# Low parts of summed weight blocks made by a negated cast and an adding DMA

## Chip, cores and metric

One core of a Trainium2 chip runs the kernel. The metric is device time in microseconds (us), the median of three executions: 2752.41 us before (2750.66 to 2753.99). The engines are called PE (TensorE), DVE (VectorE), ACT (ScalarE), POOL (GpSimd) and SP (SyncE), as in the profile.

## What is computed

The reference is one encoder block on 512 tokens with a model width of 2048:

```python
proj = rmsnorm(x, norm1_w) @ w_in          # 2048 x 9248
# 8 heads of gated DeltaNet and 8 heads of HGRN2, both directions, on columns of proj
x = x + y @ w_out                          # 2048 x 2048
h2 = rmsnorm(x, norm2_w)
x = x + (silu(h2 @ w_gate) * (h2 @ w_up)) @ w_down   # 2048 x 5632 twice, 5632 x 2048
return rmsnorm(x, norm_f_w)
```

Four stages are large matrix products: the projections by `w_in`, the output projection by `w_out`, gate and up, and the last product, "down", by `w_down`. Between the first two the heads are scanned.

## The kernel before

**The products.** Each large product is done with seven block products in place of eight (`PRODUCTS`). A **unit** is one call of `block_weights` (L957 to L978) with the matmuls that use its result. It loads 2 x 256 KB of weights into the tile `raw` by two DMAs of SP's queue, and DVE makes four blocks of sums of them in `wsum` (L972 to L974). Three raw blocks and four summed blocks are then split into a high part (`whi`, ACT casts the fp32 values to the rounded type fp32r, L976) and a low part (`wlo`, DVE subtracts the high part from the value, L977). The activations are split in the same way (`oh` and `ol`; in the projections `xh`, `xl` and `tp`). A block product is then three matmuls: high by high, high by low, low by high (L1000 to L1004). A full unit has 2 x 7 x 3 = 42 matmuls of 128x256. In the last two row blocks of down one unit in three is half as large.

**The loops.** `projections` (L313 to L427) walks over 36 groups of columns, four units each: 144 units. The output projection has 32, gate and up 176, down 96 (16 of them half units). After the last unit of a group `combine` (L1010 to L1023) adds the seven results up on DVE; in the projections the result `t` is multiplied by the row factors `rb` (L421; on POOL for the kinds k, q and v, on DVE for the others) and goes through convolution, activation and stores. POOL also multiplies in the convolution (L337), in the gates (L395) and in the preparation of the DeltaNet heads (L473, L485).

**What sets the order.** A framework schedules each engine's instructions by the program's order, priorities and its own estimate of when data are ready; the engines then run their lists in order. `block_weights` runs at a raised priority in the projections (`whead`). The pools give three buffers to `raw` and two each to `wsum`, `whi` and `wlo`, so the casts of a unit wait until the matmuls of the unit two before it have read the old contents.

Of the kernel before, what the change touches and what calls it, by code (L numbers as in the profile page):

```python
# [9 lines left out]
F32 = mybir.dt.float32  # L10
F32R = mybir.dt.float32r
U8 = mybir.dt.uint8
AF = mybir.ActivationFunctionType
ALU = mybir.AluOpType
# [3 lines left out]
P = 128  # L18
# [52 lines left out]
class Block:  # L71
# [3 lines left out]
        self.dram = ctx.enter_context(tc.tile_pool(name="dram", bufs=1, space=DRAM))  # L75

    whead = 0

    def split_act(self, src, hi, lo):
        nc = self.nc  # L80
        nc.scalar.copy(out=hi, in_=src)
        nc.vector.tensor_tensor(out=lo, in0=src, in1=hi.bitcast(F32), op=ALU.subtract)
# [230 lines left out]
    def projections(self, xops, chunk, tmp):  # L313
        nc, a = self.nc, self.a
# [83 lines left out]

        offs = dict(k=OFF_K, q=OFF_Q, v=OFF_V, z=OFF_Z, g=OFF_G, Q=OFF_QB, F=OFF_FF, B=OFF_FB, I=OFF_I)
        pend = [None, self.gates_b]  # L400
        prep = {}
        for h in range(H):
            prep.setdefault(self.PREP[h], []).append(self.gdn_head(h))
# [2 lines left out]
        n = 0  # L406
        while n < len(self.AHEAD):
            now = self.AHEAD[n:n + (2 if n == len(self.AHEAD) - 2 else 1)]
            todo = [f for m in range(n, n + len(now))
                    for f in ([pend.pop(0)] if pend else []) + ({2: [self.gates_c], 3: [self.gates_d]}.get(m, [])) + prep.get(m, [])]  # L410
            todo = [f for f in todo if f]
            prev = self.banks
            mats = [(w, (offs[kind] + g * 256, offs[kind] + g * 256 + P)) for kind, g in now]
            prods = self.block_products(mats, 0, xops, (lambda: [f(prev) for f in todo]) if todo else None, 4,
                                        before=None if n else chunk)
            self.whead = 2000
            for prod, (kind, g) in zip(prods, now):
                t = tmp.tile([P, 2, 2, ht], F32, name="t", bufs=2)
                self.combine(prod, t, tmp, 1, "comb")
                t = t.rearrange("p n h t -> p n (h t)")  # L420
                (nc.gpsimd if kind in "kqv" else nc.vector).tensor_tensor(  # L421
                    out=t, in0=t, in1=self.rb.unsqueeze(1).broadcast_to([P, 2, T]), op=ALU.mult)
                pend.append(post(kind, g, t))
            n += len(now)
        for todo in pend:
            if todo:
                todo(None)  # L427


    PREP = (18, 19, 20, 21, 23, 24, 25, 26, 22, 27)  # L430
# [366 lines left out]
    def mixers(self):  # L797
        tc = self.tc

        for n, count, shape in (("d_x0", 8, [2, P, T]), ("d_q", 4, [2, P, T]), ("d_k", 4, [2, P, T]), ("d_v", 4, [2, P, T]), ("d_g", 8, [2, P, T]),  # L800
                                ("d_hq", 4, [2, P, T]), ("d_hf", 8, [2, P, T]), ("d_hv", 4, [2, P, T]), ("d_L", 4, [2, P, 2 * T]),
                                ("d_y", 4, [4, P, T])):
            setattr(self, n, [self.dram.tile(shape, F32, name=f"{n}{i}") for i in range(count)])
        self.d_s = []
        self.banks = None
        self.wpairs, self.wbufs = 2, (3, 2, 2)
        with ExitStack() as st:
            pool = lambda name, **k: st.enter_context(tc.tile_pool(name=name, bufs=1, **k))
            early = pool("tmp0")
            acts, rest, self.smallp, self.wst = (pool(n) for n in ("acts", "tmp1", "small", "wst1"))  # L810
            tmp = Pools(rest, **{n: early for n in ("acc", "sq", "sh", "sl")})
            tops = Pools(None, **{f"tp{j}": pool(f"top{j}", side="right") for j in range(8)})
            self.ps = Banks([pool(f"ps1{i}", space=PSUM) for i in range(4)], ((0, 1), (2, 3)))
            self.tmp = tmp
            self.projections(*self.activations(tops, acts, tmp), tmp)
        self.scan()
# [140 lines left out]
    def block_weights(self, src, col):  # L957


        nc = self.nc  # L960
        n, m = src.shape[1] // 2, self.wpairs
        bufs = self.wbufs
        cut = lambda t, x: t[:, :x * n].rearrange("p (x j) n -> p x j n", j=n)
        raw = cut(self.wst.tile([P, 4 * m, P], F32, name="raw", bufs=bufs[0]), 4)
        sm = cut(self.wst.tile([P, 4 * m, P], F32, name="wsum", bufs=bufs[1]), 4)
        h = cut(self.wst.tile([P, 7 * m, P], F32R, name="whi", bufs=bufs[2]), 7)
        l = cut(self.wst.tile([P, 7 * m, P], F32R, name="wlo", bufs=bufs[2]), 7)
        with self.tc.high_priority(offset=self.whead):
            for r, c in ((2, col[0]), (0, col[1])):
                nc.sync.dma_start(out=raw[:, r:r + 2].rearrange("p k j n -> p (k j) n"), in_=src[:, :, c:c + P])  # L970
            tt = nc.vector.tensor_tensor
            tt(out=sm[:, 0:2], in0=raw[:, 0:1].broadcast_to([P, 2, n, P]), in1=raw[:, 2:0:-1], op=ALU.add)  # L972
            tt(out=sm[:, 2], in0=sm[:, 1], in1=raw[:, 2], op=ALU.add)  # L973
            tt(out=sm[:, 3], in0=sm[:, 2], in1=raw[:, 3], op=ALU.add)  # L974
            for o, src_ in ((slice(0, 3), raw[:, 1:]), (slice(3, 7), sm)):
                nc.scalar.copy(out=h[:, o], in_=src_)  # L976
                nc.vector.tensor_tensor(out=l[:, o], in0=src_, in1=h[:, o].bitcast(F32), op=ALU.subtract)  # L977
        return h, l  # L978

    def block_products(self, mats, k0, ops, between=None, at=2, order=None, before=None):  # L980


        nc = self.nc
        todo = []
        for w, col in mats:
            self.banks = self.ps.take(4, [P, 2, self.HT])
            todo.append((w.rearrange("(kt p) n -> p kt n", p=P), col, [self.banks[i // 2][:, i % 2] for i in range(7)], self.banks))
        n = KT // 2 if before else len(ops)
        starts = order or range(0, n, self.wpairs)
        for nb, j0 in enumerate(starts):  # L990
            m = min(self.wpairs, n - j0)
            if before is not None:
                before(nb)
            for v, col, prod, _ in todo:
                h, l = self.block_weights(v[:, k0 + 2 * j0:k0 + 2 * (j0 + m)], col)
                for j in range(m):
                    xh, xl = ops[j0 + j]
                    st, en = nb == 0 and j == 0, nb == len(starts) - 1 and j == m - 1
                    begun = set()
                    for wi, xi, i in self.PRODUCTS:  # L1000
                        mm = lambda a, b, s, e: nc.tensor.matmul(prod[i], lhsT=a, rhs=b, start=s, stop=e, skip_group_check=True)  # L1001
                        mm(h[:, wi, j], xh[xi], st and i // 2 not in begun, False)
                        begun.add(i // 2)
                        mm(h[:, wi, j], xl[xi], False, False)  # L1004
                        mm(l[:, wi, j], xh[xi], False, en)
            if between is not None and nb == (at - 1) // self.wpairs:
                between()
        return [banks for _, _, _, banks in todo]
# [125 lines left out]
    def run(self):  # L1134
        tc, st = self.tc, self.ctx
        pool = lambda name, where=st, side="right", **k: where.enter_context(
            tc.tile_pool(name=name, bufs=1, reuse_waits="tile", **(dict(side=side) if side else {}), **k))
        self.constants()
        self.mixers()
        self.ps = Banks([pool(f"ps{i}", side=None, space=PSUM) for i in range(4)], ((0, 2), (1, 3)))  # L1140
        self.wpairs, self.wbufs = 2, (3, 2, 2)
        self.wst = pool("wst")
        self.io = pool("io")
        self.ops = [pool("ops0", side="left"), pool("ops1", side="left")]
        self.ops.append(self.ops[1])
        with ExitStack() as ffn:
            self.ops.append(pool("ops3", ffn))
            self.sums = pool("sums", ffn)
            self.xops = []
            with ExitStack() as late:  # L1150
                token_scale = self.out_proj(pool("late", late))
            tio = pool("tio", side="left")
            self.gate_up(token_scale, pool("tb", ffn))
        self.down(tio, pool("more", side="left"), pool("accs"), pool("dtmp"))


# [19 lines left out]
```

## Time and profile before

| | |
|---|---|
| median of three executions | 2752.41 us |
| the profiled execution: its time | 2746.68 us |
| its span, first to last instruction | 2744.9 us |
| busy in the span: PE, DVE, ACT, POOL | 2520.9, 2506.7, 1282.1, 296.4 us |
| mean granted TensorE clock | 0.963 of 2.4 GHz |
| DMA read and written, mean rate | 361.89 MB, 132 GB/s |

An engine's busy time is the time in which it runs an instruction. Matmuls are pipelined, and the profile models their ends, so a stretch in which PE reads as busy throughout can still be slower than PE at its peak; the spacing of the matmuls tells that. The stages of this kernel follow one another, so each is read from its own stretch of the span: the projections fill it up to about 892 us, the scans lie between 892 and 1201 us, output projection, gate and up between 1201 and 2265 us, and down follows to the end.

### The profile page before, as it was taken

What the parts mean: (1) busy time and instruction counts of PE and PEld (TensorE: products, weight loads), DVE (VectorE), ACT (ScalarE), POOL (GpSimd) and SP (SyncE); (2) the same over time, 40 slices, a digit from 0 to 9 for tenths busy, and PEclk for the clock granted to TensorE, in tenths of its full rate; (3) what the DMA queues carried; (4) which work ended last, traced back from release to release, by engine and by line L of the source; (5) the groups of instructions that cost most, each with busy time, mean ns of one, the idle gap of its engine ahead of it and who ended that gap; (6) DMA issues with size and microseconds to landing.
All of it is one profiled execution on the core that took longest, in us unless ns stands there. A gap on an engine that the chain in (4) does not pass through costs nothing.

```text
span 2744.9 us, 55187 instructions
## 1 busy us (share of the span) xinstructions
PE 2520.9 (92%) x22511; PEld 2449.8 (89%) x22511; DVE 2506.7 (91%) x3978; ACT 1282.1 (47%) x1777; POOL 296.4 (11%) x148
## 2 busy tenths in 40 slices
PE   6999999888899587889999999999999999899996
PEld 5989999888899476789899999999999999898996
DVE  8999999998999887889998989999899999999996
ACT  6555655445454443444644434344433443444444
POOL 0121112223112554210000000000000000000000
PEclk9999999999999798999999999999999999999998
DMA  6334344556444643546434443434344364434333
GB/s 185 109 101 130 109 132 111 164 156 167 118 143 135 203 134 90 166 145 181 147 114 128 121 124 116 123 119 121 116 124 123 110 200 144 131 106 126 107 93 100
DMA packets 562345, 361.89 MB, mean 132 GB/s; under 512 B 51393, under 2 KB 514683, under 8 KB 562091
## 3 DMA queue, kind: packets, MB, share of 16 engines
q1 hardware_dynamic: 543515, 311.70, 39.6%
q10 hardware_dynamic: 18576, 46.67, 4.8%
q8 instruction: 176, 2.88, 0.4%
q14 instruction: 78, 0.64, 0.1%
HBM read 303.66 MB, written 54.62 MB: 131 GB/s over the span
## 4 chain that ended last, share of the span: by engine, by line
PE 49%; DVE 15%; issue 6%; DMA 4%; ACT 2%; POOL 1%; POOLq 0%; SPq 0%; ACTq 0%; DVEq 0%
PE big L1001 46%; DVE wlo L977 4%; DVE ol L954 1%; DVE wsum L972 1%; DVE wsum L974 1%; DMA L<-d_L 1%; DVE wsum L973 1%; ACT whi L976 1%; POOL acc L473 1%; DVE X L744 1%; DVE X L746 1%; DMA acc<-d_rows 0%; DVE lt L517 0%; DVE tsum L937 0%; PE oT L628 0%
## 5 line engine op out<-in xcount | busy, mean ns | idle before, releaser
L1001 PE MATMUL big<-oh,whi 128*128 128x256 f32 x4144 | 1139.1, 284 | 31.7 <-ACT whi L976 21.1
L1001 PE MATMUL big<-ol,whi 128*128 128x256 f32 x4144 | 1139.5, 282 | 1.8 <-DVE ol L954 1.6
L1001 PE MATMUL big<-oh,wlo 128*128 128x256 f32 x4144 | 1070.6, 283 | 16.8 <-DVE wlo L977 16.4
L1001 PEld LDWEIGHTS big<-oh,whi 128*128 128x128 f32 x4144 | 783.5, 190 | 42.4 <-ACT whi L976 28.8
L976 ACT CAST whi<-raw 128x768 fp32r<-128x768 f32 (+1 forms) x448 | 368.9, 824 | 907.3 <-PE big L1001 649.9
L1001 PEld LDWEIGHTS big<-ol,whi 128*128 128x128 f32 x4144 | 785.6, 190 | 3.3 <-DVE ol L954 2.8
L1001 PEld LDWEIGHTS big<-oh,wlo 128*128 128x128 f32 x4144 | 746.7, 190 | 22.6 <-DVE wlo L977 21.8
L977 DVE TENSOR_TENSOR wlo<-wsum,whi 128x1024 fp32r<-128x1024 f32 (+1 forms) x448 | 542.1, 1210 | 9.5 <-ACT whi L976 9.3
L976 ACT CAST whi<-wsum 128x1024 fp32r<-128x1024 f32 (+1 forms) x448 | 462.0, 1032 | 151.2 <-DVE wsum L974 148.1
L977 DVE TENSOR_TENSOR wlo<-raw,whi 128x768 fp32r<-128x768 f32 (+1 forms) x448 | 432.7, 966 | 85.9 <-ACT whi L976 82.2
L1001 PE MATMUL big<-tp,whi 128*128 128x256 f32 x2304 | 415.0, 286 | 27.9 <-ACT whi L976 17.0
L1001 PEld LDWEIGHTS big<-tp,whi 128*128 128x128 f32 x2304 | 348.5, 193 | 33.6 <-ACT whi L976 19.6
L972 DVE TENSOR_TENSOR wsum<-raw 128x512 f32<-128x512 f32 (+1 forms) x448 | 313.3, 700 | 10.2 <-DMA raw<-in_w_in 3.1
L1001 PE MATMUL big<-tp,wlo 128*128 128x256 f32 x1152 | 293.5, 290 | 21.7 <-DVE wlo L977 21.4
L1001 PE MATMUL big<-xh,whi 128*128 128x256 f32 x864 | 246.1, 289 | 10.4 <-ACT whi L976 7.3
L1001 PE MATMUL big<-xl,whi 128*128 128x256 f32 x864 | 244.8, 287 | 0.0
L1001 PE MATMUL big<-xh,wlo 128*128 128x256 f32 x864 | 229.3, 287 | 4.6 <-DVE wlo L977 4.3
L1001 PEld LDWEIGHTS big<-tp,wlo 128*128 128x128 f32 x1152 | 206.8, 195 | 28.8 <-DVE wlo L977 28.3
L974 DVE TENSOR_TENSOR wsum<-wsum,raw 128x256 f32<-128x256 f32 (+1 forms) x448 | 206.9, 463 | 2.4
L973 DVE TENSOR_TENSOR wsum<-wsum,raw 128x256 f32<-128x256 f32 (+1 forms) x448 | 189.4, 424 | 3.6
L1001 PEld LDWEIGHTS big<-xh,whi 128*128 128x128 f32 x864 | 167.7, 194 | 12.3 <-ACT whi L976 8.4
L1001 PEld LDWEIGHTS big<-xl,whi 128*128 128x128 f32 x864 | 166.7, 193 | 0.5
(302 smaller groups left out, 2628.2 us busy)
## 6 DMA issues: line engine op xcount, KB each, us to landing
raw<-in_w_in SPq DMA_DIRECT2D x288, 256.0 KB, 3.4
raw<-in_w_gate SPq DMA_DIRECT2D x176, 256.0 KB, 3.3
raw<-in_w_up SPq DMA_DIRECT2D x176, 256.0 KB, 3.4
raw<-in_w_down SPq DMA_DIRECT2D x160, 256.0 KB, 3.3
raw<-in_w_out SPq DMA_DIRECT2D x64, 256.0 KB, 4.2
d_t<-yt ACTq DMA_DIRECT2D x22, 512.0 KB, 4.1
tt<-d_t ACTq DMA_DIRECT2D x22, 512.0 KB, 4.0
d_x<-tp SPq DMA_DIRECT2D x16, 256.0 KB, 4.9
```

What stands on the lines that cost most here:

```text
L473: nc.gpsimd.tensor_tensor(out=gb, in0=gb, in1=gc, op=ALU.subtract)
L744: nc.vector.tensor_tensor(out=xv[:, 0:2, n, 0, :], in0=xv[:, 0:2, n, 0, :], in1=tv[:, :, n, 1:2].broadcast_to([P, 2, nb // 2, hs]), op=ALU ...
L746: nc.vector.tensor_tensor(out=xv[:, 2:4, n, 1, :], in0=xv[:, 2:4, n, 1, :], in1=tv[:, :, n, 0:1].broadcast_to([P, 2, nb // 2, hs]), op=ALU ...
L954: nc.vector.tensor_tensor(out=o, in0=src, in1=hh.bitcast(F32), op=ALU.subtract)
L972: tt(out=sm[:, 0:2], in0=raw[:, 0:1].broadcast_to([P, 2, n, P]), in1=raw[:, 2:0:-1], op=ALU.add)
L973: tt(out=sm[:, 2], in0=sm[:, 1], in1=raw[:, 2], op=ALU.add)
L974: tt(out=sm[:, 3], in0=sm[:, 2], in1=raw[:, 3], op=ALU.add)
L976: nc.scalar.copy(out=h[:, o], in_=src_)
L977: nc.vector.tensor_tensor(out=l[:, o], in0=src_, in1=h[:, o].bitcast(F32), op=ALU.subtract)
L1001: mm = lambda a, b, s, e: nc.tensor.matmul(prod[i], lhsT=a, rhs=b, start=s, stop=e, skip_group_check=True)
```

## The change

In the projections and in down, the low parts of the four summed blocks no longer come from DVE. ACT writes the negated rounded value into the low tile, and a DMA of POOL's queue adds the fp32 sums to it in place; the result is again the value less its rounded part. The raw blocks keep their way. The high and low tiles are cut in two, raw (`whr`, `wlr`) and sums (`whs`, `wls`), with two buffers each, and `wsum` gets a third buffer. Within a unit the three raw products of both pairs come first and the four summed ones after them, in all stages. The multiplication by `rb` is always on DVE. The memory reserved for the descriptors of POOL's DMAs is set to 4096 bytes in each partition.

```diff
-                (nc.gpsimd if kind in "kqv" else nc.vector).tensor_tensor(
+                nc.vector.tensor_tensor(
                     out=t, in0=t, in1=self.rb.unsqueeze(1).broadcast_to([P, 2, T]), op=ALU.mult)
...
-        self.wpairs, self.wbufs = 2, (3, 2, 2)
+        self.wpairs, self.wbufs = 2, dict(raw=3, wsum=3, whr=2, whs=2, wlr=2, wls=2)
...
-            for o, src_ in ((slice(0, 3), raw[:, 1:]), (slice(3, 7), sm)):
-                nc.scalar.copy(out=h[:, o], in_=src_)
-                nc.vector.tensor_tensor(out=l[:, o], in0=src_, in1=h[:, o].bitcast(F32), op=ALU.subtract)
-        return h, l
+            for hi, lo, src_, by_dma in ((hr, lr, raw[:, 1:], False), (hs, ls, sm, True)):
+                if by_dma and self.dma_lo:
+
+                    nc.scalar.mul(out=lo, in_=src_, mul=-1.0)
+                    nc.scalar.copy(out=hi, in_=src_)
+                    nc.gpsimd.dma_start(out=lo.rearrange("p x j n -> p (x j n)").bitcast(F32),
+                                        in_=src_.rearrange("p x j n -> p (x j n)"), accum_op=ALU.add)
+                else:
+                    nc.scalar.copy(out=hi, in_=src_)
+                    tt(out=lo, in0=src_, in1=hi.bitcast(F32), op=ALU.subtract)
...
+                begun = set()
+                for part in (self.PRODUCTS[:3], self.PRODUCTS[3:]):
+                    for j in range(m):
+                        xh, xl = ops[j0 + j]
+                        en = nb == len(starts) - 1 and j == m - 1
+                        for wi, xi, i in part:
...
+                            mm(h[wi][:, j], xh[xi], nb == 0 and i // 2 not in begun, False)
+                            begun.add(i // 2)
+                            mm(h[wi][:, j], xl[xi], False, False)
+                            mm(l[wi][:, j], xh[xi], False, en)
...
+        self.dma_lo = True
         self.down(tio, pool("more", side="left"), pool("accs"), pool("dtmp"))
...
-    nc = bacc.Bacc("TRN2", target_bir_lowering=False, num_devices=1)
+    nc = bacc.Bacc("TRN2", target_bir_lowering=False, num_devices=1, dynamic_dma_scratch_size=4096)
```

`dma_lo` is also set at the start of the loop over the projections' groups and cleared at its end.

ACT in the projections, between the second and third group of columns, before (the numbers at the tiles' names are the program's; one unit's `whi` is one number):

```order
L976 CAST whi_1733<-wsum_1732 128x1024
L343 ACTIVATE sq_1349<-acc_1333 128x1024
L309 ACTIVATE sig_1478<-ba_716 32x512
L81 CAST sh_1351<-sq_1349 128x1024
L976 CAST whi_1788<-raw_1786 128x768
L976 CAST whi_1788<-wsum_1787 128x1024
L320 ACTIVATE sig_1600<-t_1591 128x1024
```

and the same place after:

```order
L980 ACTIVATE wls_1790<-wsum_1786 128x1024
L985 CAST whr_1845<-raw_1843 128x768
L344 ACTIVATE sq_1385<-acc_1369 128x1024
L310 ACTIVATE sig_1520<-ba_725 32x512
L82 CAST sh_1387<-sq_1385 128x1024
L981 CAST whs_1846<-wsum_1844 128x1024
L980 ACTIVATE wls_1848<-wsum_1844 128x1024
L985 CAST whr_1938<-raw_1936 128x768
```

A unit has three casts on ACT in place of two, and the scheduler puts the high part of the sums (`whs`) ahead of the negated cast (`wls`) that the DMA waits for.

POOL at the same place in the projections, before:

```order
L421 TENSOR_TENSOR t_1324<-t_1324,rb_732 128x1024
L337 TENSOR_TENSOR acc_1333<-acc_1333,sig_1344 128x1024
L421 TENSOR_TENSOR t_1841<-t_1841,rb_732 128x1024
L337 TENSOR_TENSOR acc_1850<-acc_1850,sig_1861 128x1024
L421 TENSOR_TENSOR t_2346<-t_2346,rb_732 128x1024
```

and after:

```order
L982 DMA wls_1528<-wsum_1524 128x1024
L982 DMA wls_1586<-wsum_1582 128x1024
L982 DMA wls_1664<-wsum_1660 128x1024
L982 DMA wls_1722<-wsum_1718 128x1024
L338 TENSOR_TENSOR acc_1369<-acc_1369,sig_1380 128x1024
L982 DMA wls_1790<-wsum_1786 128x1024
```

POOL now issues 240 adding DMAs (144 in the projections, 96 in down), and 36 multiplications of the projections (L337, L395, L473, L485 of before) stand between them in its list.

PE within one unit of the projections, after (`whr_1787` belongs to the next unit):

```order
L1012 MATMUL big_1656<-tp2_410,whs_1720 128x256 x2
L1012 MATMUL big_1655<-tp2_410,whs_1720 128x256 x2
L1012 MATMUL big_1657<-tp2_410,whs_1720 128x256 x2
L1012 MATMUL big_1658<-xh_212,whr_1787 128x256
L1012 MATMUL big_1658<-xl_213,whr_1787 128x256
...
L1012 MATMUL big_1656<-tp2_410,wls_1722 128x256
L1012 MATMUL big_1655<-tp2_410,wls_1722 128x256
L1012 MATMUL big_1657<-tp2_410,wls_1722 128x256
L1012 MATMUL big_1657<-xh_212,whs_1720 128x256
L1012 MATMUL big_1657<-xl_213,whs_1720 128x256
L1012 MATMUL big_1657<-xh_212,wls_1722 128x256
```

Six matmuls with the high parts of the sums and the first of the next unit's raw products stand ahead of the first matmul that reads the DMA's result. From there to the unit's last read of `wls` it is 18 matmuls.

## Rows read from the trace of the kernel before

**Rows 1.** The page's first part: span, then busy time, share, instructions of engines
```profile
span 2744.9 us, 55187 instructions
PE 2520.9 (92%) x22511; PEld 2449.8 (89%) x22511; DVE 2506.7 (91%) x3978; ACT 1282.1 (47%) x1777; POOL 296.4 (11%) x148
```

**Rows 2.** Windows of three stages: length, engines' busy time, granted clock, DMA share, rate
```profile
70.00:892.00 822.00, 760.17 (x6078) 744.06 (x6077) 774.69 (x1189) 436.40 (x517) 162.09 (x53) 0.97 0.47 131
...
1201.00:2265.00 1064.00, 1049.18 (x8729) 1041.41 (x8730) 978.89 (x1481) 458.85 (x560) 0.00 (x0) 0.99 0.44 132
2265.00:2745.00 480.00, 430.98 (x3509) 421.58 (x3507) 444.68 (x749) 211.62 (x392) 0.00 (x0) 0.96 0.39 115
```

**Rows 3.** Timeline in gate and up: start, duration, engine, instruction [idle before]
```profile
1600.35 0.28 PE L1001 MATMUL big<-ol,whi 128*128 128x256 f32 x1
...
1600.35 0.84 ACT L976 CAST whi<-raw 128x768 fp32r<-128x768 f32 x1 [3.20 <-PE big L1001]
1600.46 0.28 PE L1001 MATMUL big<-oh,wlo 128*128 128x256 f32 x1
...
1605.30 0.83 ACT L976 CAST whi<-raw 128x768 fp32r<-128x768 f32 x1 [3.15 <-issue]
```

**Rows 4.** Groups of instructions, 70 to 892 us: busy, mean ns, idle before
```profile
L977 DVE TENSOR_TENSOR wlo<-wsum,whi 128x1024 fp32r<-128x1024 f32 x138 | 173.2, 1255 | 7.1 <-ACT whi L976 6.9
...
L976 ACT CAST whi<-wsum 128x1024 fp32r<-128x1024 f32 x139 | 145.6, 1047 | 75.6 <-DVE wsum L974 75.1
...
L421 POOL TENSOR_TENSOR t<-t,rb 128x1024 f32<-128x1024 f32 x12 | 42.0, 3504 | 240.1 <-DVE t L1023 238.2 <-issue 1.9
L337 POOL TENSOR_TENSOR acc<-acc,sig 128x1024 f32<-128x1024 f32 x12 | 35.6, 2967 | 152.9 <-ACT sig L322 134.4 <-DVE wlo L977 18.5
...
L473 POOL TENSOR_TENSOR acc<-acc,gcol 128x1024 f32<-128x1024 f32 x8 | 30.4, 3795 | 90.6 <-DMA acc<-d_rows 51.2 <-ACT comb L1018 13.7 <-ACT whi L976 13.4
L421 DVE TENSOR_TENSOR t<-t,rb 128x1024 f32<-128x1024 f32 x22 | 28.9, 1313 | 0.0
...
L485 POOL TENSOR_TENSOR sh<-sh,acc 128x1024 f32<-128x1024 f32 x8 | 20.0, 2497 | 24.5 <-DVE wlo L977 10.5 <-ACT acc L475 8.2 <-ACT sig L320 5.8
...
L469 PE MATMUL big<-acc 128*128 128x128 f32 x64 | 9.6, 293 | 1.4 <-ACT comb L1018 1.4
```

**Rows 5.** Waits, 70 to 892 us: who waited for whom, total us, times, longest
```profile
ACT whi L976 <- PE big L1001: 194.6, 94, 7.3
...
PE big L1001 <- DVE wlo L977: 24.4, 30, 2.8
PE big L1001 <- ACT whi L976: 24.3, 13, 5.1
```

**Rows 6.** Groups of instructions in down, 2265 to 2745 us
```profile
L1001 PE MATMUL big<-oh,whi 128*128 128x256 f32 x1148 | 314.2, 284 | 13.5 <-ACT whi L976 8.7 <-ACT junk L1128 1.7 <-DVE tsum L1019 1.1
...
L1001 PE MATMUL big<-oh,wlo 128*128 128x256 f32 x1149 | 280.3, 284 | 12.2 <-DVE wlo L977 11.9
...
L977 DVE TENSOR_TENSOR wlo<-wsum,whi 128x1024 fp32r<-128x1024 f32 x74 | 89.9, 1217 | 1.3 <-ACT whi L976 1.3
```

**Rows 7.** DMA issues, 70 to 892 us: queue, count, size, median us from issue to landing
```profile
acc<-d_rows SPq DMA_DIRECT2D x8, 512.0 KB, 6.1
...
d_g<-sig ACTq DMA_DIRECT2D x7, 512.0 KB, 3.0
...
d_l<-ld SPq DMA_DIRECT2D x8, 64.0 KB, 1.8
```

**Rows 8.** SP's own time to issue a load of `raw`: ns, shortest, median, longest
```profile
L970 SPq DMA_DIRECT2D raw<-in_w_gate x12: 368/438/512, 1502.8 to 1547.9; - x12
```

**Rows 9.** A POOL instruction that only writes, in the scans
```profile
L545 POOL MEMSET P<- 128x1024 f32 x8 | 7.4, 952 | 11.0 <-PE sc L649 11.0
```

## Prediction before the change was run

> **What bounds the kernel now.** I read the page's busy times first, then the windows by stage, then a few us of the timeline where PE never stops, then the groups and waits of the projections and of down. Over the whole span PE is 92% busy and DVE 91% [rows 1]. That average hides that the stages differ. From 1201 to 2265 us PE is busy 1049 of 1064 us: there PE is the bound, and nothing done for DVE can gain more than 15 us [rows 2]. In the projections PE is busy 760 of 822 us and DVE 775, in down 431 and 445 of 480 [rows 2]: the two engines stop each other.
>
> What PE needs at its best is read in gate and up. Two casts of raw blocks, one unit apart, start at 1600.35 and 1605.30, so a full unit takes 4.95 us; that is 42 matmuls at 0.118 us, and neighbouring rows of PE are 0.11 to 0.12 us apart [rows 3]. In the projections' window there are 139 casts of sums, so 139 units [rows 4]: 139 x 4.95 = 688 us. The other 6078 - 139 x 42 = 240 instructions of PE cost about 0.15 us each, going by 64 of them in 9.6 us [rows 2, 4]: 36 us. PE's floor is 724 us, and **98 us** of the 822 can be won at most. As a cross-check, PE reads as idle for 62 us, and a granted clock of 0.97 means some 6% of the time, 49 us, at 1.2 GHz, which loses another 25 us [rows 2]: 87 us. The waits say why PE stops: 24.4 us for DVE's `wlo` and 24.3 us for ACT's `whi` [rows 5]. In down the same two kinds of wait are 12.2 and 13.5 us, together **26 us** [rows 6].
>
> **The change part by part.**
>
> *DVE loses work.* In the projections' window 138 subtractions of 1.255 us go, 173 us; 12 multiplications by `rb` come from POOL at 1.31 us each, 16 us [rows 4]. DVE's 775 us become 617, below PE's floor of 724. In down 74 x 1.217 = 90 us of its 445 go [rows 2, 6]. So DVE stops being a bound in both stages. POOL loses 12 x 3.5 = 42 us [rows 4].
>
> *ACT gains a cast.* The nearest row is the cast of the same sums, 1.05 us [rows 4]. 139 of them are 146 us, and ACT's 436 us become 582 of at least 724: covered in sum. The cost is in the order. ACT already waits 194.6 us for PE inside its list, because a cast needs the buffer of the unit two before it [rows 5], and it now waits there twice in a unit, with sigmoids and other work queued behind.
>
> *The chain of the adding DMA* is the term on which all rests. The trace has no adding DMA and no DMA of POOL's. The chain begins when PE has read the old `wls` for the last time. Then follow the `whs` cast and the negated cast, 2 x 1.05 = 2.1 us; the bound below is 1.05, if `whs` is done by then [rows 4]. POOL's issue: SP needs 0.44 us for one, which is the bound below; a POOL instruction that only writes 512 KB takes 0.95 us, and the longest multiplication 3.8 us, the bound above [rows 4, 8, 9]. I take 0.95, since writing descriptors is nearest to an instruction that only writes. The transfer: a plain 512 KB store lands in 3.0 us, the bound below; a slow 512 KB load takes 6.1 us, the bound above [rows 7]. Between 64 KB (1.8 us) and 512 KB (3.0 us) each further 512 KB cost 1.4 us [rows 7]; the adding DMA reads its target as well as its source, so I take 3.0 + 1.4 = 4.4 us. The sum is **7.45 us**, with ends at 1.05 + 0.44 + 3.0 = 4.5 and 2.1 + 3.8 + 6.1 = 12.0 us.
>
> A price that only a page has: the Trainium skill, in "DMA: Bandwidth & Descriptors", section "Latency and other measured facts", gives about 1 us to the first byte for a DMA of POOL's queue and about 0.6 for the others. By that the issue would cost 0.44 + 0.4 = 0.84 us, the chain would be 7.3 us and the forecast the same; no run here shows it yet.
>
> *What covers the chain.* Two `wls` buffers mean that the chain may last from a unit's last read to the first read two units on. Of the 84 matmuls of two units 18 lie between the first and the last read of `wls`, as PE's list shows, so 66 x 0.118 = **7.8 us** are left. The chain of 7.45 us just fits. If it does not, two units take chain + 2.1 us in place of 9.9.
>
> *What does not fit.* The margin is 0.35 us, so disturbances show. POOL runs in order: 36 multiplications of 2.5 to 3.8 us stand between the DMAs, some waiting for ACT or a load themselves [rows 4]. If a third of them delay a DMA by one multiplication, 12 x 2.7 = 32 us are lost; I take 30, with ends at 0 and 36 x 2.8 = 100. For ACT's order I take 20 us, with ends at 0 and 75 (half a us in each unit).
>
> *Raw products first, split tiles, a third `wsum`.* In gate and up PE is full, so these cost and give nothing there; the bounds are +5 and the 15 us of idle time [rows 2]. In the other stages the order is already in the 7.8 us; the third buffer covers the time that the DMA reads `wsum`.
>
> *The sum.* Projections: -98 + 30 + 20 = -48. Down: of the 26 us I give back 14 for units at the borders of row blocks, where ACT also casts activations: -12. Together -60. The profiled execution took 2746.7 us, so 2686.7; the median of the three runs lies 5.7 above it, so **2692 us**.
>
> **Rivals.**
>
> *A. The chain is shorter.* If the transfer costs no more than a plain store, the chain is 6.05 us, and nearly all idle time goes: -98 - 26 + 10 = -114, or 2638 us. For it: 3.0 us stores are common [rows 7]. Against: the target must be read too.
>
> *B. The DMA engines become the bound.* Their share in the projections is 0.47 of 822 us, 386 us [rows 2]. At 1.4 us of all engines for each 512 KB read [rows 7], 139 adding DMAs take 195 us if only one stream counts and 389 if both do. 386 + 389 = 775 us is above PE's floor of 724; if the engines cannot be kept over 95% busy, the stage lasts 816 us, and loads and adding DMAs queue behind one another. Down has 0.39 x 480 + 81 x 2.8 = 414 of 480 us and gains nothing. The total is then near 2745 us. By the Trainium skill, "DMA: Bandwidth & Descriptors", section "Issuing engines are not separate DMA queues", POOL's DMAs run on the same 16 engines as SP's loads and interleave with them, so a queue of its own gives no relief. For this rival: that the stage has the higher share of the two. Against: no window read here is over half full [rows 2].
>
> *C. The chain is too long (slower).* The place is PE's first read of `wls`. With a chain of 10 us two units take 12.1 us, 6.06 each. Projections: 139 x 6.06 = 842 against 822, +20. Down: 73 full units x 1.1 us, 16 half ones x 0.6, less the 26 us of idle time: +64. The total is 2752 + 84 = 2836 us. At 11 us it is near 2945. It decides from about 9.3 us, where 794 us in the projections (-28) meet some +35 in down. For it: the ends of the three unknown prices reach 12.0 us, and loads of 256 KB for two units always run beside the transfer. Against: only slow prices together get there.
>
> *D. POOL's list is the new wait.* If nearly all 36 multiplications hold a DMA back, 100 us go, and -98 - 26 + 100 + 20 is about no change: 2748 us.
>
> That the change doesn't do what it says I leave at nothing: all 240 DMAs and casts stand in the lists.
>
> **How the numbers follow.** Chances: forecast 0.43, A 0.10, B 0.12, C 0.28, D 0.07. A measurement of this kernel tells about 0.2% from no change, 5.5 us. Faster by more: the forecast, A and two thirds of B, 0.61. Within it: the rest of B and half of D, 0.07. Slower: C and the rest of D, 0.32. The forecast's own range is 2640 to 2735. Faster and slower hold most of the chance together, so the range goes from just under A, 2630, to the lower half of C, 2820; it leaves out a few per cent below and about 14 above.
>
> **What would show it.** Right: subtractions of sums gone from DVE, its busy time in the projections near 617 us, that stage some 48 us shorter, PE's waits for `wlo` gone and small new waits for the DMA into `wls`; POOL's DMAs landing in 4 to 5 us. Wrong: PE waiting for that DMA in most units, landing times over 6 us, down longer than 480 us (C); a DMA share near 0.9 (B); POOL's DMAs waiting behind multiplications (D).

## The result: 5% slower, and the profile after

The changed kernel takes **2893.45 us** (median of four runs, 2887.42 to 2898.8) against 2752.34 in the runs beside it: ratio 1.0512, 95% interval 1.0488 to 1.0536. The forecast was 2692 us, in a range from 2630 to 2820. The profiled execution took 2887.42 us.

First the page: busy times, DMA share by slice, and the queues; q0 holds POOL's adding DMAs.

```profile
PE 2562.3 (89%) x22511; PEld 2479.0 (86%) x22511; DVE 2249.9 (78%) x3750; ACT 1511.3 (52%) x2017; POOL 425.2 (15%) x376
...
DMA  7899998889899643455444344434343589888876
...
q1 hardware_dynamic: 543515, 311.70, 37.3%
q0 software_dynamic: 34560, 121.65, 23.4%
```

DVE has lost 257 us and ACT gained 229, as meant [rows 1]; and PE is idle for longer. The DMA share is eight or nine tenths wherever adding DMAs run, the first third and the end of the span.

Windows of the projections (to their last matmul) and of down (length, busy times, granted clock, DMA share, rate), of the changed kernel:

```profile
70.00:951.00 881.00, 776.94 (x6173) 757.28 (x6173) 641.99 (x1071) 568.94 (x662) 215.70 (x185) 0.96 0.89 210
2334.00:2885.60 551.60, 462.87 (x3631) 448.76 (x3629) 376.13 (x677) 297.63 (x493) 80.21 (x93) 0.94 0.83 190
```

The same two stages of the kernel before, cut in the same way:

```profile
70.00:900.00 830.00, 767.12 (x6133) 750.68 (x6133) 781.93 (x1198) 440.73 (x522) 164.71 (x57) 0.97 0.47 133
2248.00:2744.90 496.90, 447.98 (x3653) 438.58 (x3652) 461.12 (x776) 218.85 (x401) 0.00 (x0) 0.96 0.41 123
```

In down PE's idle time grows from 49 to 89 us (551.60 - 462.87), and its busy time by 15 us for about as many matmuls, at a granted clock of 0.94 for 0.96. The waits of the changed kernel in its projections, where before there were 24.4 us for `wlo` and 24.3 for `whi` [rows 5]:

```profile
DVE wsum L974 <- DMA wls<-wsum: 118.6, 65, 5.8
...
PE big L1012 <- DMA wls<-wsum: 52.7, 41, 4.8
DVE wsum L974 <- DMA raw<-in_w_in: 44.2, 20, 4.9
```

and in its down:

```profile
DVE wsum L974 <- DMA wls<-wsum: 98.1, 57, 3.8
...
PE big L1012 <- DMA wls<-wsum: 55.4, 37, 4.7
```

Its DMA issues (KB each, median us to landing, counted from the start of the issue): an adding DMA takes 5.7 us, and loads beside it a full us longer than before.

```profile
wls<-wsum POOLq DMA_DIRECT2D x224, 512.0 KB, 5.7
raw<-in_w_in SPq DMA_DIRECT2D x288, 256.0 KB, 4.4
...
raw<-in_w_down SPq DMA_DIRECT2D x160, 256.0 KB, 4.3
```

Where the time went is read from the first load of each weight tensor, the last store of `d_t` (the end of gate and up) and the span. One table for all runs, in us. "Sums" is the number of `wsum` buffers, "PE waits" PE's waits for adding DMAs in the whole span.

| run | sums | to first `w_out` load | out proj. | gate and up | down | PE waits | median |
|---|---|---|---|---|---|---|---|
| before | 2 | 1120.0 | 193.5 | 934.9 | 496.5 | none | 2752 |
| the change | 3 | 1171.6 | 196.2 | 965.9 | 551.9 | 116.8 | 2893 |
| e1 no adds | 3 | 1126.0 | 195.7 | 959.6 | 498.6 | none | 2784 |
| e2 third `whs`, `wls` | 3 | 1230.5 | 196.4 | 974.1 | 576.2 | 40.6 | 2984 |
| e3 adds in down | 3 | 1125.8 | 200.7 | 962.4 | 548.9 | 58.3 | 2840 |
| e4 copies in down | 3 | 1123.7 | 199.7 | 960.9 | 495.1 | 23.3 | 2780 |
| e5 adds, old order | 3 | 1218.1 | 203.1 | 1031.7 | 602.7 | 175.8 | 3058 |
| e6 no adds, old order | 3 | 1151.8 | 202.3 | 1018.4 | 507.6 | none | 2883 |
| e7 no adds, mixed order | 3 | 1130.9 | 198.0 | 1020.7 | 504.9 | none | 2860 |
| e8 dummy adds of sums | 3 | 1230.8 | 195.8 | 969.0 | 560.7 | none | 2958 |
| e9 no adds | 2 | 1123.2 | 183.9 | 937.2 | 500.5 | none | 2745 |
| e10 no adds, old order | 2 | 1111.2 | 197.5 | 936.0 | 496.7 | none | 2744 |
| e11 the change | 2 | 1195.5 | 197.0 | 935.4 | 560.0 | 131.3 | 2894 |
| e12 five `raw` | 3 | 1185.0 | 183.4 | 946.0 | 553.3 | 120.0 | 2869 |
| e13 dummy adds of highs | 2 | 1173.4 | 200.1 | 937.7 | 513.6 | none | 2828 |
| e14 every second unit | 2 | 1225.4 | 192.0 | 938.7 | 570.6 | 167.3 | 2930 |
| e15 every fourth unit | 2 | 1162.7 | 190.9 | 937.4 | 531.0 | 82.8 | 2824 |
| e16 half adds | 3 | 1172.0 | 195.9 | 967.5 | 535.1 | 85.7 | 2867 |
| e17 half adds | 2 | 1224.0 | 195.1 | 935.7 | 579.9 | 141.1 | 2941 |
| e18 half adds in down | 2 | 1115.9 | 194.0 | 936.7 | 564.7 | 53.5 | 2816 |

The change's span is 140.7 us longer: 51.6 up to the output projection, 2.7 there, **31.0 in gate and up, where no adding DMA runs**, and 55.4 in down.

### The profile page after: what moved, and what is told of

Read it like the earlier page. It is cut to its first block, busy times and chain, and to the rows that moved or that the text cites. A ratio compares the mean times of both kernels' runs of the same rounds, so it can differ in the third digit from the quotient of the medians.

```text
span 2885.6 us, 56418 instructions
## 1 busy us (share of the span) xinstructions
PE 2562.3 (89%) x22511; PEld 2479.0 (86%) x22511; DVE 2249.9 (78%) x3750; ACT 1511.3 (52%) x2017; POOL 425.2 (15%) x376
## 4 chain that ended last, share of the span: by engine, by line
PE 35%; DMA 26%; DVE 17%; issue 15%; ACT 4%; POOL 2%; SPq 2%; ACTq 0%; DVEq 0%; POOLq 0%
PE big L1012 30%; DMA wls<-wsum 15%; DMA raw<-in_w_gate 3%; DVE wlr L986 3%; DMA raw<-in_w_up 2%; DVE wls L986 2%; DVE wsum L974 2%; ACT wls L980 2%; DVE wsum L975 1%; DMA raw<-in_w_in 1%; DVE ol L957 1%; DVE wsum L976 1%; SPq L972 1%; PE oT L631 1%; PE sc L652 1%
## 5 line engine op out<-in xcount | busy, mean ns | idle before, releaser
L1012 PE MATMUL big<-oh,wls 128*128 128x256 f32 x2368 | 649.4, 288 | 76.1 <-DMA wls<-wsum 64.2
L1012 PE MATMUL big<-oh,whs 128*128 128x256 f32 x2368 | 662.1, 284 | 2.3 <-ACT whs L985 1.2
L1012 PE MATMUL big<-ol,whs 128*128 128x256 f32 x2368 | 661.1, 283 | 0.0
L974 DVE TENSOR_TENSOR wsum<-raw 128x512 f32<-128x512 f32 (+1 forms) x448 | 310.2, 692 | 416.8 <-DMA wls<-wsum 224.1
L1012 PEld LDWEIGHTS big<-oh,wls 128*128 128x128 f32 x2368 | 442.2, 193 | 91.2 <-DMA wls<-wsum 59.5
L1012 PE MATMUL big<-oh,whr 128*128 128x256 f32 x1776 | 501.4, 285 | 20.3 <-ACT oh L955 14.2
L1012 PE MATMUL big<-oh,wlr 128*128 128x256 f32 x1776 | 494.5, 283 | 8.3 <-DVE wlr L986 8.1
L1012 PE MATMUL big<-ol,whr 128*128 128x256 f32 x1776 | 499.2, 283 | 2.6 <-DVE ol L957 2.5
L986 DVE TENSOR_TENSOR wlr<-raw,whr 128x768 fp32r<-128x768 f32 (+1 forms) x448 | 424.3, 947 | 43.9 <-ACT whr L985 43.3
L1012 PEld LDWEIGHTS big<-oh,whs 128*128 128x128 f32 x2368 | 453.6, 192 | 4.2 <-ACT whs L985 1.8
L1012 PEld LDWEIGHTS big<-ol,whs 128*128 128x128 f32 x2368 | 454.1, 192 | 0.0
L1012 PEld LDWEIGHTS big<-oh,wlr 128*128 128x128 f32 x1776 | 335.0, 191 | 11.3 <-DVE wlr L986 11.1
```

What stands on the lines that cost most here:

```text
L986: tt(out=lo, in0=src_, in1=hi.bitcast(F32), op=ALU.subtract)
```

## Experiments

**First: traffic, buffers, or the order?** T says that the adding DMAs fill the engines; C that their chain is too long for two buffers; O that raw-first costs by itself.

e1, no adds:

```diff
-        self.dma_lo = True
+        self.dma_lo = False
```

> The change with the adding DMA switched off everywhere: DVE subtracts all low parts again; raw products first, split tiles, third wsum buffer and the multiplication by rb on DVE stay. If only the adding DMA cost time (theories T, the DMA engines are full, and C, the chain through two buffers is too long), the whole returns to 2745 to 2760 us. If the order with raw products first costs time of its own (theory O, from the 31 us that gate and up lost without any adding DMA), gate and up stay some 30 us longer than before and the total is 2775 to 2790 us.

Measured 2783.92 us, ratio 1.0124 (1.0093 to 1.0156). So 110 us come with the adds; the remaining 31 without them, of which 25 in gate and up.

e2, three buffers for the summed high and low parts:

```diff
-dict(raw=3, wsum=3, whr=2, whs=2, wlr=2, wls=2)
+dict(raw=3, wsum=3, whr=2, whs=3, wlr=2, wls=3)
```

> The change with three buffers in place of two for the high and low parts of the sums (whs, wls). The chain from a unit's last read of wls may then last some 5 us longer. C: PE's waits for the adding DMA (53 us in the projections, 55 in down) go, the projections fall from 951 to below 900 us on the time axis, total 2790 to 2830 us. T: the DMA share stays near 0.9 and the total stays at 2875 to 2900 us.

2983.89 us, slower still. PE's waits for adds did shrink, but DVE's list now waits for loads instead:

```profile
DVE wsum L974 <- DMA raw<-in_w_in: 217.8, 83, 7.2
DVE wsum L974 <- DMA raw<-in_w_down: 147.5, 63, 6.1
...
PE big L1012 <- DMA wls<-wsum: 40.6, 26, 2.7
```

I took this as the end of C. That was too early: the edit had moved DVE's list as well.

e3, adds in down alone (`dma_lo` stays False in the projections), and e4, there with a plain copy (it leaves the addition out, so down's low parts are not low parts):

```diff
-                                        in_=src_..., accum_op=ALU.add)
+                                        in_=src_...)
```

> The adding DMA in down alone. All theories: projections back to about 900 us, down some 55 us longer than before; with O gate and up 30 us longer as well: 2835 to 2845 us; without O about 2810 us. It is the control for the next run.

> As the run with the adding DMA in down alone, but the DMA copies the sums over the negated parts and does not add (the low parts of down's sums are then not low parts). The target is not read any more. T: one such DMA takes about half the time of all DMA engines (1.4 us for 512 KB in place of 2.9), down's DMA share falls from 0.83 to about 0.6, the landing from 5.6 to about 4 us and down gets 30 to 55 us shorter than with the adding DMA. If reading the target costs nothing, time, share and landing stay.

2840.44 and 2779.74 us. The queue of POOL's DMAs and their landing, of e3:

```profile
q0 software_dynamic: 13824, 46.14, 9.3%
...
wls<-wsum POOLq DMA_DIRECT2D x80, 512.0 KB, 5.6
```

and of e4:

```profile
q0 software_dynamic: 12800, 46.14, 4.4%
...
wls<-wsum POOLq DMA_DIRECT2D x80, 512.0 KB, 3.8
```

For the same bytes the add takes twice the engine time and lands 1.8 us later, and down goes from 548.9 to 495.1 us. Both traffic and chain became smaller here, so it doesn't tell T from C. It is the nearest that a run comes to rival A: with landings of 3.8 us PE still waits 23.3 us for the copies, and down, at 495.1 us, is 3.5 us shorter than in e1 and 1.4 shorter than before, where A counted on 26.

**Second: what costs 31 us in gate and up?** e5 and e6 put the loop over `j` outside again, with adds and without; e7 keeps raw-first in the projections alone, without adds.

```diff
-                for part in (self.PRODUCTS[:3], self.PRODUCTS[3:]):
-                    for j in range(m):
+                for part, j in [(self.PRODUCTS, j) for j in range(m)]:
+                    if True:
```

> The changed kernel with its adding DMAs, but with the products of a unit in the order of before (first pair of rows: all 21 matmuls, then the second pair), everywhere. Theory T (the adding DMA fills the 16 DMA engines, every load lands later) and theory O (the order raw products first, by itself, costs the 31 us that are lost between the projections and down, where no adding DMA runs): gate and up go back to 934.9 us from the first gate load to the last store (965.9 in the changed kernel), projections and down stay near +51 and +55, or worse, since a low part of a sum is asked for after 9 matmuls instead of 18; the total 2860 to 2890 us. If the order matters nowhere, 2893 us.

> No adding DMA, products in the order of before; what is left of the change is the four split weight tiles, the third buffer of the sums and the scaling of the projections moved from POOL to DVE. If the order raw-first costs by itself what the run without adding DMAs lost against before (2784 against 2750): about 2750 us, gate and up 935 us. If the split tiles or buffers cost it: about 2784 us, gate and up 960 us.

> No adding DMA; raw products first in the projections alone, the order of before in the output projection, gate and up, and down. By O the 25 us lost in gate and up come back: 2750 to 2760 us; the projections end near 885 us as in the run without adding DMAs (900 before), and what comes of these 15 us later is open, since the scans gave them back in that run: 2735 us if they don't here.

3058.07, 2882.73 and 2859.89 us: all three missed, and on the side that refutes O. With the old order gate and up take 1018 to 1032 us; raw-first had *hidden* part of a loss. The timeline of e6 in gate and up shows it, here DVE and PE:

```profile
1699.62 0.69 DVE L974 TENSOR_TENSOR wsum<-raw 128x512 f32<-128x512 f32 x1 [0.83 <-DMA raw<-in_w_up]
1700.23 1.22 DVE L1065 TENSOR_TENSOR yt<-yt,u 128x1024 f32<-128x1024 f32 x1
1701.36 0.95 DVE L986 TENSOR_TENSOR wlr<-raw,whr 128x768 fp32r<-128x768 f32 x1
...
1702.37 0.39 PE L1012 MATMUL big<-oh,wlr 128*128 128x256 f32 x1 [0.83 <-DVE wlr L986]
```

The sums of a later unit stand in DVE's list ahead of this unit's low part and wait 0.83 us for their load; PE then waits 0.83 us for the low part. Over gate and up of e6 the sums wait 179 us for their loads, and PE 53 us for DVE's low parts. Theory W: the third `wsum` buffer lets the schedule place them there. Two buffers again, without adds (e9; e10 with the old order too) and with them (e11); e12 gives `raw` five buffers instead.

```diff
-dict(raw=3, wsum=3, whr=2, whs=2, wlr=2, wls=2)
+dict(raw=3, wsum=2, whr=2, whs=2, wlr=2, wls=2)
```

> Without adding DMAs, raw products first, and the sums back to two buffers as before (split weight tiles and the scaling on DVE stay). Theory W: the third buffer of the sums lets the sums of a later unit come ahead of this unit's low parts in DVE's list, where they wait for their raw load (73 + 27 us of DVE waits for raw loads in gate and up of the run with three, 2 us or none before) and hold the low parts that PE needs; then gate and up go back to 935 us (959.6 with three) and the time to 2735 to 2760 us. If the split tiles or the order of the products cost it: 2784 us and waits for raw loads as before.

> Without adding DMAs, products in the order of before, two buffers of sums: only the split weight tiles and the scaling on DVE are left of the change. W: 2745 to 2765 us, against 2883 with three buffers of sums. If the split tiles cost it: 2850 to 2883 us.

> The changed kernel, but two buffers of sums. W: gate and up (965.9 us in the change) go back to about 935 us. In projections and down the two theories stand against each other: a sum's buffer comes free only when the adding DMA has read it (DVE waited 119 and 98 us for that with three), so two buffers should cost there; T alone gives no loss there. Total 2855 us if nothing is lost there, 2900 to 2960 us if the buffer is what the DMA needs.

> The changed kernel with five buffers of raw blocks for three, so that loads start two units earlier. If sums wait in DVE's list for raw loads that land late (45 us of DVE waits in projections, 67 us in gate and up), these waits go: gate and up back to about 935 us, projections 20 to 40 us shorter, total 2820 to 2860 us. If the list of DVE or the filled DMA engines set the time whatever the lead: 2880 to 2900 us.

2744.66, 2743.87, 2894.31 and 2868.92 us. **W is shown**: every run with two buffers of sums has gate and up at 935 to 939 us, every one with three and three raw buffers at 959 or more, whatever the order, and in gate and up of e9 and e10 the waits of `wsum` for raw loads are gone, but for 0.3 us; PE's waits for DVE's low parts fall to 2 and 5 us. Earlier loads (e12) get 20 of the 31 us back; where the other 11 come from stays open. But e11 gains nothing in all: the stretch up to the output projection becomes 24 us longer and down 8, since there the third buffer is what lets DVE go on while a DMA still reads the sums (DVE's waits for that rise from 224.1 to 283.0 us). Against before, e9 and e10 are at 0.9983 (0.9967 to 0.9999) and 0.9978 (0.9962 to 0.9994), a gain of some 0.2%, too small to build on.

**Third: traffic or waiting?** e8 keeps DVE's low parts and lets as many adds run into a tile that nothing reads; e13 does so with two buffers of sums and the high parts as source, so that no sum waits either. The cut shows e13; e8 reads the sums (`sm`).

```diff
+            if self.dma_lo:
+                self.nd = (self.nd + 1) % 2
+                nc.gpsimd.dma_start(out=self.dummy[:, self.nd, :4 * n * P], in_=hs..., accum_op=ALU.add)
```

> The adding DMAs run as often and with as many bytes, in projections and down, each after its sums and into a tile that nothing reads; low parts come from DVE as in before, and no instruction of ACT, DVE or PE waits for an adding DMA, but the buffer of a sum comes free only after it. Otherwise as the run without adding DMAs (2784 us). Theory T: the DMA engines' share in projections is near 0.9 again and the loads land as late, so most of the 110 us between that run and the changed kernel are there: 2840 to 2900 us. If the chain behind each adding DMA (casts, POOL, transfer, matmuls) were what costs: 2780 to 2800 us.

> The run without adding DMAs with two buffers of sums (2745 us), and beside it the adding DMAs of projections and down as dummies: as many, with as many bytes, but they read the high parts, whose buffers PE holds for longer anyway, and add into a tile that nothing reads. So no low part and no sum waits for them; only their traffic, POOL's issues and DVE's full work on low parts are there. Theory T (the traffic itself, which makes every load land later): share of the DMA engines near 0.85 in projections, in_w_in and in_w_down land in 4 us or more (3.4 and 3.3 without), projections and down some 50 us longer each, 2830 to 2880 us. Theory C2 (traffic is harmless while nobody waits for its end; what costs in the change is that low parts and the sums' buffers wait for it): loads still in time, 2745 to 2775 us.

2958.06 and 2828.38 us. e8 is above even T's range, but the third buffer is in it: DVE's sums wait 158 us for loads of `w_in` and `w_down` (22 in e1), and only 8 for their buffers. e13 against e9 is the cleaner pair; its total lies just under T's range, its stages don't agree with one another. Windows of e13, projections and down:

```profile
70.00:938.00 868.00, 781.48 (x6140) 763.07 (x6138) 775.67 (x1211) 437.57 (x522) 243.17 (x184) 0.95 0.88 210
2311.00:2824.80 513.80, 449.26 (x3606) 439.50 (x3605) 459.19 (x773) 220.92 (x399) 80.36 (x93) 0.94 0.87 206
```

and of e9:

```profile
70.00:895.00 825.00, 765.36 (x6141) 747.42 (x6140) 785.60 (x1211) 438.17 (x522) 105.80 (x45) 0.98 0.48 134
2244.00:2744.80 500.80, 446.63 (x3608) 437.67 (x3606) 458.51 (x774) 221.36 (x400) 0.00 (x0) 0.95 0.41 121
```

At a DMA share of 0.87 or more, with no low part and no sum waiting, the projections lose 43 us (868 - 825) and down 13. But something does wait for these adds, the cast that needs the buffer they read:

```profile
ACT whs L988 <- DMA dummy<-whs: 46.8, 22, 5.9
```

Of this 33.9 us are in the projections and 13.0 in down, so 43 and 13 us are at most what traffic and POOL's issues cost. The change with two buffers of sums (e11) loses 60 in down. So in down most of the loss is something that e13 doesn't have. ACT's extra cast is not it, since e4 has it too and its down took 495.1; the waits for the adds are left. In the projections traffic and POOL's issues can be at most 43 of e11's 79 us (904 against 825).

e14 and e15: adds in every second and every fourth unit, with two buffers of sums (the cut shows e15).

```diff
-                if by_dma and self.dma_lo:
+                if by_dma and self.dma_lo and self.nunit % 4 == 0:
```

> Two buffers of sums, raw products first, adding DMAs in every second unit of projections and down only. The DMA engines' time in projections is then about 386 + 195 us for some 820: share 0.7. If queueing at a full set of DMA engines is what costs, most of the cost goes and DVE's relief (half of 157 us there) shows: 2700 to 2745 us. If each adding DMA costs its wait (as C2 has it): half of the 150 us between the runs with two buffers of sums with and without the adds: about 2820 us.

> As the run before this, but every fourth unit. Full engines as the cause: share 0.6, 2720 to 2745 us. Each adding DMA costs its wait: about 2782 us.

2929.8 and 2824.43 us, both above the dearer of their two expectations. Windows of e15:

```profile
70.00:941.00 871.00, 783.10 (x6145) 760.43 (x6146) 747.73 (x1177) 472.60 (x560) 130.90 (x80) 0.96 0.56 148
2291.00:2822.00 531.00, 450.45 (x3605) 439.56 (x3603) 436.89 (x748) 241.49 (x423) 20.72 (x24) 0.94 0.51 136
```

and its waits for adds, and their landing:

```profile
PE big L1014 <- DMA wls<-wsum: 82.8, 40, 5.7
...
wls<-wsum POOLq DMA_DIRECT2D x56, 512.0 KB, 6.2
```

With the engines half empty, a quarter of the adds still costs 46 us in the projections and 30 in down. Full engines are not needed for the loss: T as the sole cause fell. An add lands no sooner in a half-empty set of engines (6.2 us for 5.7), and 60 adds make PE wait 40 times. What is later here is the start of the chain. Take each unit's last read of the old low part, its cast, its DMA and its next read in order: in the projections the negated cast ends, in the median, 2.3 us after that read in e11, 3.3 in e14 and 5.3 in e15, and the add lands 8.7, 9.9 and 12.2 us after it. So where adds alternate with DVE's subtractions each add costs PE more because its cast comes late; whether ACT's list or late sums hold the cast back stays open.

**Fourth: the same bytes in two halves**, two sums each, the products of the first half ahead (e16; e17 with two buffers of sums; e18 in down alone).

```diff
+                    for q in (slice(0, 2), slice(2, 4)):
+                        nc.gpsimd.dma_start(out=lo[:, q]..., in_=src_[:, q]..., accum_op=ALU.add)
...
-                for part in (self.PRODUCTS[:3], self.PRODUCTS[3:]):
+                for part in (self.PRODUCTS[:3], self.PRODUCTS[3:6:2], self.PRODUCTS[4:7:2]):
```

> The changed kernel with each adding DMA cut into two, of two sums each, and the products of the two sums of the first half ahead of those of the second (raw, then sums 3 and 4, then sums 5 and 6): same bytes, so the same traffic, twice POOL's issues, but the first half lands about 2 us sooner after the cast (3.4 to 3.7 us for the 256 KB adds against 5.7) and the second half has 12 more matmuls, 1.4 us, of cover. C2 (the wait for each adding DMA's end is what costs): PE's waits for the adds (117 us in the change) fall below 40 us, 2820 to 2860 us. T (traffic): 2890 us or more.

> The same with two buffers of sums, beside the run of the change with two buffers (2894). C2: 2790 to 2850 us, near the run in which nothing waits for the dummy adds (2828). T: 2890 us or more.

> Adding DMAs in halves, in down alone, two buffers of sums, everything else as in the run without adds (2745 us, down 500 us). The dummy adds cost 13 us in down, the adds of the change 52 to 60 us. C2: down 500 to 520 us, 2745 to 2765 us in all; with the forecast's gain of DVE in down besides, 2733 us. T: 2795 us or more.

2866.55, 2941.03 and 2816.42 us: e16 lies between its two expectations, e17 and e18 on T's side. But the edit didn't shorten the chain as meant: half the bytes land after 5.2 us in place of 5.7. The sixteen adds of 256 KB that stand alone in the change's down land after 3.4 us, so it is not the size that keeps the halves late; that it is their standing in pairs, two issues of POOL in 1.75 us, is not shown. So a short chain at full traffic stays untried, and the three runs are inconclusive on it.

## Why the prediction was wrong, step by step

**The chain: right mechanism, wrong size.** The first step that failed is "just fits": 7.45 us of chain against 7.8 of cover. The timeline of the changed kernel in down shows one, here ACT, POOL and PE:

```profile
2505.57 0.28 PE L1012 MATMUL big<-oh,wls 128*128 128x256 f32 x1
...
2505.82 1.05 ACT L981 CAST whs<-wsum 128x1024 fp32r<-128x1024 f32 x1 [1.90 <-PE big L1012]
2506.78 1.05 ACT L980 ACTIVATE wls<-wsum 128x1024 fp32r<-128x1024 f32 x1
...
2508.57 0.86 POOL L982 DMA_DIRECT2D wls<-wsum  x1 [6.44 <-DVE tsum L1030]
...
2514.68 0.62 PE L1012 MATMUL big<-oh,wls 128*128 128x256 f32 x3 [1.35 <-DMA wls<-wsum]
```

PE's last read of the old low part ends at 2505.85. The two casts take 2.0 us, as forecast; POOL, which had been idle, starts 0.7 us later; from the start of its issue to PE's read it is 6.1. Together 8.8 us, and PE stands for 1.35. The next chain through the same buffer, from 2517.07 to 2525.09, takes 8.0 us and stalls PE for 0.89. Over all units of the two windows (matched in order, from the last read to the landing) the median chain is 8.4 us in the projections, with 87 of 140 over the cover, and 8.0 in down, with 50 of 93 over it; the means are 8.8 and 8.2.

By terms: a landing is counted from the start of the issue. So the store's 3.0 us [rows 7] held its own issue already, and the forecast put issue and transfer together at 0.95 + 4.4 = 5.35 us; the adds of 512 KB measured 5.7 (4.5 to 11.1), of which the issue is 0.87. From the cast's end to POOL's issue nothing was put; it took 0.3 us in the median. These two make some 0.6 us. The rest is spread, in the casts' start and above all in the landings, a quarter of which take over 6.6 us in the projections; PE pays for those. The order of the casts was right.

**Rival C's deciding point was wrong too.** Its price began at 9.3 us on average, as if a short chain could pay for a long one; by it the measured means of 8.8 and 8.2 us would still have been a gain. A short one can't pay: PE loses on each late landing and gets nothing for an early one, and landings spread over 6.6 us. PE waited 41 times in the 139 units of the projections' window and 37 times in the 96 of down, 108 us in sum. Its 842 us at a chain of 10 us is also short of the 36 us of other matmuls that the floor counts; with them it is 878, and the price begins near 9.0.

The sums of PE's waits go along with what the adds cost in some pairs, run against the same kernel without them: 117 us of waits and 110 of time in the change, 58 and 57 in e3, 176 and 175 in e5 (against e6), 83 and 80 in e15, 131 and 150 in e11, 167 and 185 in e14 (these three against e9). The halves have their own order of products and so no exact twin; beside e1 and e9 they show 86 and 83 (e16), 141 and 196 (e17), 54 and 72 (e18). Other runs break this row: 41 and 200 in e2, none and 174 in e8, none and 84 in e13, 23 and no cost in e4. So waiting is not the whole.

**Rival B: sized right, priced wrong.** Its engine time was put at 775 us in the projections; it is 0.89 x 881 = 784. One add costs all engines 0.234 x 2885.6 / 232 = 2.9 us (224 full and 16 half ones), 2.8 forecast for two streams. The Trainium skill, "DMA: Bandwidth & Descriptors", section "Issuing engines are not separate DMA queues": POOL's DMAs interleave with SP's loads on the same engines. By that rule a queue of its own keeps the adds out of no load's way, and the trace agrees: loads land in 4.4 us for 3.4. But I let traffic cost nothing below a 95% share. e13 puts it, with POOL's issues, at up to 43 us in the projections and 13 in down, at 0.88 and 0.87.

**"These cost and give nothing" in gate and up** failed, with bounds of +5 and -15 us: +31. PE was full there, but a full PE only means nothing to win. I counted the third `wsum` buffer as cover, and did not read what it does to DVE's list in the stage where PE has no slack. Nor does it "cover the time that the DMA reads `wsum`" in the other stages: DVE waits 118.6 and 98.1 us there, 65 and 57 times, until a DMA lets go of a buffer.

**DVE, ACT, POOL.** DVE 642 us in a longer window (617 forecast), ACT 569 (582): right. D was rightly given little: of the 140 adds in the projections' window 8 were issued more than 1 us after their cast's end, and of POOL's 571 us of idle time before its issues 373.5 were spent waiting for ACT's cast. Whether the gains of 98 and 26 us would have reached the total is open: without adds (e1) the projections end 21 us sooner than before (809 against 830 us), and the scans give it back, the first `w_out` load coming 6 us later than before. That a gain in the projections is a gain in the total was a term that the sum took without a reason.

**The sum.** Forecast -48, 0 and -12; measured +51.6 (up to the first `w_out` load), +31.0 and +55.4 (and 2.7 in the output projection). The +31.0 are shown to come from the third buffer. The other two come with the adds: e15 shows that full engines are not needed for a loss there, and e13 that part of it comes without any wait of PE or DVE for an add. What stays open: how much of the projections' loss is traffic on loads, and how much POOL's added issues among its other work; and what a truly shorter chain would give.

## What to carry to other kernels

Where work goes from an engine to a DMA, compare the *spread* of the whole chain with the cover, not the mean alone: PE pays for each late one, and average slack is no cover. Price an adding DMA in engine time as twice a plain one. A buffer more is an edit of the schedule too: read the lists of stages that it was not meant for, and try it alone.

## What the runs showed that I had not expected

- An adding DMA takes twice a plain copy's time on the engines: 46.14 MB took 9.3% of the 16 engines' span of 2837.8 us in e3, 4.4% of 2779.4 in e4, 3.0 against 1.4 us for each 512 KB; landing 5.6 against 3.8 us.
- An add's landing hardly depends on the fill of the engines: 5.7 us at a share of 0.89, 6.2 at 0.56 with a quarter of the adds. Size does count: 3.4 us for the 256 KB adds that stand alone, though 5.2 for those issued in pairs.
- A third buffer of one tile costs 22 us in a stage that PE had filled (e1 against e9 with raw-first), 31 with adds in the stages beside it (the change against e11), and 82 with the old order (e6 against e10).
